# Attention loop: running maximum folded to 256 columns ahead of the last score bank, and value products placed by head

## The chip, the core and the metric

The kernel runs on one core of a Trainium2 chip. A core has five engines that run side by side, each with its own queue of instructions, and that wait for one another by semaphores: TensorE (PE in the profile; its weight loads are PEld), VectorE (DVE), ScalarE (ACT), GpSimd (POOL) and SyncE (SP, which here issues DMAs). SBUF is the working memory, PSUM the accumulator into which TensorE writes. The metric is the device time of one execution in microseconds (us), the lower the better; runs of one kernel are given by their median.

## The reference, cut to what matters

The program is a two-layer network over 1024 latent tokens and 256 context tokens. Each layer projects its input, runs four groups side by side (latent attention, a pooling mixer, a state space, a gating block) and projects the result. The change lies in the attention alone, which is this, for blocks of queries:

```python
def one(qs):
    qn, qr = qs
    s = (jnp.einsum('bqhd,bkhd->bhqk', qn, k_nope)
         + jnp.einsum('bqhr,bkr->bhqk', qr, k_rope))
    p = jax.nn.softmax(s.astype(jnp.float32) * scale, axis=-1)
    return jnp.einsum('bhqk,bkhd->bqhd', p, vf)
```

There are 4 heads with 64 value columns each. Latent queries look at all 1280 keys (10 blocks of 128), context queries (first layer only) at the 256 context keys. All is in float32.

## The kernel before

`attention` (line 1200) works on 256 queries and two heads at a time: a *pair* is one group of 256 queries with heads 0 and 1, or with heads 2 and 3. The first layer has 10 pairs, 8 of latent queries and 2 of context queries, the second layer 8. The loop at line 1465 makes one turn for each head of each pair: `v` is the pair, `h` the head in it (0 the first, 1 the second). In this text the turns are numbered through both layers: 0 to 19 in the first, 20 to 35 in the second. Turns 4, 5, 18 and 19 belong to context queries and are short (2 key blocks); the other 32 are long (10 key blocks).

Scores are kept turned: keys on the partitions, queries along the columns. A *bank* of PSUM holds 512 columns, here two key blocks of 256 queries each, so a long turn has 5 banks (`BANKS`, line 1198). The softmax needs the maximum over all keys of each query. The order of a turn, by names and lines:

- `scores` (line 1300): TensorE writes the scores bank by bank, 6 matmuls in each (line 1316, tiles `mm_sc` or `tp_sc`). The first bank of a turn is computed at the end of the turn before, and ScalarE copies it to `acc`, an SBUF tile of 128 x 512 (line 1322). For each of the other four banks VectorE takes the elementwise maximum of `acc` and the bank (line 1324; in the profile these stand under line 130, the helper that issues them, as `acc<-acc,mm_sc`). Behind the last bank VectorE folds `acc` to 256 columns: the maximum of its two halves, both in SBUF (line 1326, in the profile `acc<-acc`).
- `maxima` (line 1333): TensorE transposes the folded `acc` (line 1338, tile `tp_mx`), and VectorE reduces it to one maximum a query, `mx` (line 1340).
- `rows` (line 1342): TensorE turns `mx` back and spreads it out (line 1347, again tile `tp_mx`), and VectorE makes `row` of it in two instructions (lines 1349 and 1350; 143 and 147 in the profile).
- `shift` (line 1352): TensorE adds `row` to each score bank with one more matmul, which subtracts the maximum.
- `exps` (line 1361): ScalarE takes the exponentials of the five banks (`pE`, `pL`, `pM`), and GpSimd adds them up to `psum`: four adds of 512 columns and one fold to 256, all operands in SBUF (lines 1383 and 1384; line 130 in the profile).
- `values` (line 1388): TensorE multiplies the exponentials of the **pair before** with the values, into `av`, 64 x 256 each. There are 10 key blocks and 2 heads, so 20 such products for a pair; they are given out over the two turns of the next pair as something for TensorE to do while VectorE works on the maximum. `PVS` (line 36) says how: the 5 key blocks of a turn are cut into three pieces, put ahead of `maxima`, between `maxima` and `rows`, and between `rows` and `shift` (lines 1482 to 1489). A product of one key block and head is one matmul in the program and two records in the profile. In the first pair of a layer `att_values` stands there in their place, and `PVS` is not used; nor does it do anything where the pair before is short.

Ahead of `maxima` there may also be matmuls for the queries of the next pair (tile `tp_q`). Within the loop the order on TensorE, VectorE, ScalarE and GpSimd is the order in which the code issues (`manual_schedule`, line 1464): each engine takes its instructions strictly one after the other.

Of the kernel before, what the change touches and what calls it, by code (L numbers as in the profile page):

```python
# [16 lines left out]
ALU = mybir.AluOpType  # L17
# [15 lines left out]
NSLOT = 160  # L33
NPOS = 165
SEG = 32
PVS = ((0, 2), (2, 3), (3, 5))
VW = ((0, 1, None), (2, 3, None))
CX = 2
POW = ((0, 4), (4,))
# [35 lines left out]
def tile_hybrid_backbone(ctx: ExitStack, tc: tile.TileContext, A):  # L75
    nc = tc.nc
    V, S, P, T, D = nc.vector, nc.scalar, nc.gpsimd, nc.tensor, nc.sync
# [23 lines left out]
    def mm_ps():  # L101
        return psmm.tile([128, 512], F32, tag="mm", name="mm_" + stg[0])

    def tp_ps():
        return pstp.tile([128, 512], F32, tag="tp", name="tp_" + stg[0])
# [16 lines left out]
    def s2(name="s2", dt=F32):  # L122
        return wk.tile([128, 512], dt, tag="s2", name=name, bufs=2)
# [5 lines left out]
    def tt(e, out, a, b, op):  # L129
        return e.tensor_tensor(out=out, in0=a, in1=b, op=op)  # L130
# [1069 lines left out]
    def attention(l, last, blocks, out):  # L1200
# [5 lines left out]
        n = 256  # L1206
# [21 lines left out]
        def q_split(c0):  # L1228
            ts_ = slice(c0, c0 + n)
            cqn = (xs("cqn", F32R, 1024) if len(chunk) == 1 else hx("cqn", F32R)).rearrange("p (k e t) -> p k e t", k=2, e=2)  # L1230
            parts = [(cqn[:, 0], cq0[:, ts_]), (cqn[0:64, 1], cq1[0:64, ts_])]
            rope = None
            if c0 < NLAT:
                rope = tile_of("ropeq", F32, 2)
                D.dma_start(rope, A["rope"][:, :, ts_])
            chunk[c0] = cqn, rope
            yield "act"
            for y, x in parts:
                S.copy(y[:, 0], x)
            S.copy(cqn[64:128, 1, 0], cqn[0:64, 1, 0])  # L1240
            yield "dve"
            for y, x in parts:
                sub(P, y[:, 1], x, y[:, 0])

        def q_chunk(c0):

            cqn, rope = chunk[c0]
            yield "mm"
            stg[0] = "q"
            ps = tp_ps()  # L1250
            q_mm(ps[:, 0:n], cqn, slice(256, 384))
            if c0 < NLAT:
                q_mm(ps[:, n:2 * n], cqn, slice(384, 512))
            yield "act mm"
            qf = wl("qf", F32)
            m = 2 * n if c0 < NLAT else n
            S.copy(qf[:, 0:m], ps[:, 0:m])
            yield "row"
            if c0 < NLAT:
                mul(V, qf[:, 0:m].rearrange("p (e t) -> p e t", e=2), qf[:, 0:m].rearrange("p (e t) -> p e t", e=2), rope)  # L1260
                add(V, qf[:, 0:n], qf[:, 0:n], qf[:, n:2 * n])
            qr = tile_of("qr", F32R, 2)
            chunk[c0] = cqn, qr
            yield "act"
            S.copy(qr[:, 0], qf[:, 0:n])
            yield "dve"
            sub(V, qr[:, 1], qf[:, 0:n], qr[:, 0])
# [32 lines left out]
        def scores(v, h, banks):  # L1300

            c0, pr = pairs[v]
            stg[0] = "sc"
            K, Q = KT[2 * pr + h][(slice(0, 96), slice(0, 128))[h]], prep[v][h]
            if 0 in banks:
                st[v, h] = dict(b=[], acc=s2("acc"))
            d = st[v, h]
            acc = d["acc"]
            for i, kts in list(enumerate(BANKS if c0 < NLAT else BANKS[0:1]))[banks.start:banks.stop]:
                ps = tp_ps() if nb[0] % 6 == 5 else mm_ps()  # L1310
                nb[0] += 1
                d["b"].append(ps)
                for x, kt_ in enumerate(kts):
                    out = ps[:, n * x:n * x + n]
                    for y, (e, f) in enumerate(((0, 0), (0, 1), (1, 0))):
                        T.matmul(out, lhsT=K[:, e, 128 * kt_:128 * kt_ + 128], rhs=Q[:, f], start=(x == 0 and y == 0),  # L1316
                                 stop=False, skip_group_check=True)
                if c0 == NLAT:
                    V.tensor_reduce(out=acc[:, 0:n], in_=ps.rearrange("p (x q) -> p q x", x=2), axis=AX.X, op=ALU.max)
                    continue  # L1320
                if i == 0:
                    d["first"] = lambda: S.copy(acc, d["b"][0])
                else:
                    tt(V, acc, acc, ps, ALU.max)
                if i == 4:
                    tt(V, acc[:, 0:n], acc[:, 0:n], acc[:, n:2 * n], ALU.max)

        def first(v, h):

# [79 lines left out]
        def finish(v):  # L1409

            c0, pr = pairs[v]
            ci = min(c0 // 512, 2)
            gt = c0 - CH0[ci][0]
            gs = G[ci][:, pr, gt:gt + n]
            yield "fend"
            stg[0] = "sm"
            tp = tp_ps()
            for h in range(2):
                T.matmul(tp[64 * h:64 * h + 64, 0:n], lhsT=ones.to_broadcast([128, 64]), rhs=st[v, h]["sm"][:, 0:n],
                         start=True, stop=True, skip_group_check=True)  # L1420
            yield "fdve"
            rs = qp[0].tile([128, n], F32, tag="rs", name="rs", bufs=2) if v < nv - 1 else s2("rs")[:, 0:n]
            V.reciprocal(out=rs, in_=tp[:, 0:n])
            yield "av"
            mul(V, gs, st[v][:, 0:n], gs)
            mul(V, gs, rs, gs)
            for x in (v, (v, 0), (v, 1)):
                st.pop(x)
# [3 lines left out]
        def start(g):  # L1432
            work.append([next(g), g])

        def go(what):

            for x in list(work):
                if x[0] == what:
                    x[0] = next(x[1], None)
                    if x[0] is None:  # L1440
                        work.remove(x)
# [22 lines left out]
        with tc.manual_schedule(engines={mybir.EngineType[x] for x in MAN}):  # L1464
            for w in range(2 * nv):
                v, h = w // 2, w % 2
                short = pairs[v][0] == NLAT
                for u in fresh[1:]:
                    if w == max(2 * u - 5, 0):
                        start(q_split(pairs[u][0]))  # L1470
                go("act")
                scores(v, h, range(1, 5))
                if h == 0 and v:
                    start(finish(v - 1))
                for u in fresh[1:]:
                    if w == 2 * u - 3:
                        start(q_chunk(pairs[u][0]))
                if h == 0 and v + 1 < nv:
                    start(q_pair(v + 1, *pairs[v + 1]))
                go("mm")  # L1480
                go("act mm")
                k = [range(5 * h + i, 5 * h + j) for i, j in PVS]
                vals(v, w, k, 0)
                maxima(v, h)
                vals(v, w, k, 1)
                rows(v, h)
                go("m4")
                go("row")
                vals(v, w, k, 2)
                if h and short:  # L1490
                    go("fend")
                    go("fdve")
                if h:
                    go("av")
                if not short:
                    go("fend")
                    go("fdve")
                go("dve")
                if w == 2 * nv - 2:
                    out.y(0)  # L1500
                if w == 2 * nv - 1:
                    drop("attq", "att")
                    out.alloc()
                    out.split()
                shift(v, h)
                if w + 1 < 2 * nv:
                    scores((w + 1) // 2, 1 - h, range(0, 1))
                exps(v, h)
                if w == 2 * fresh[-1] - 3:
                    out.scales()  # L1510
                if w == 2 * nv - 4:
                    out.load()
                    out.load()
                if w == 2 * nv - 2 and short:
                    for _ in range(3):
                        out.load()

            v = nv - 1
            go("act")
            start(finish(v))  # L1520
            out.part(0)
            values(v, range(0, 4))
            out.split()
            out.part(0)
            out.load()
            out.load()
            values(v, range(4, 10))
            out.split()
            go("fend")
            go("fdve")  # L1530
            go("av")
            out.load()
            out.load()
            out.load()
            out.part(0)
            out.split()
            out.part(0)
            out.split()
            out.part(0)
# [500 lines left out]
```

## Time and profile before

| | us |
|---|---|
| median of 3 runs | 1385.57 |
| the runs | 1374.05, 1385.57, 1389.56 |
| the profiled execution, its own time | 1387.97 |
| its span, first to last instruction | 1386.2 |
| attention loop, first layer (turns 0 to 19) | about 455 to 645 |
| attention loop, second layer (turns 20 to 35) | about 1119 to 1280 |
| TensorE, VectorE, GpSimd busy over the span | 1270.6, 899.5, 412.9 |
| granted TensorE clock, mean share of full speed | 0.961 |

The profile shows one execution. A row of its timeline is: start, duration (both us), engine, line, operation, what it writes and reads, and how often; instructions of one kind that follow each other are merged into one row, whose duration goes from the first one's start to the last one's end. In brackets stands how long the engine was idle before it and who ended the wait. Matmuls overlap in the array, and their ends are modelled: a matmul may start some 0.07 us before the end that is shown for the one in front.

### The profile page before, as it was taken

Reading aid. Unit: us, or ns where it says so; the run is one execution under the profiler, and the core shown is the slowest. Engines: PE = TensorE matmul, PEld = TensorE weight load, DVE = VectorE, ACT = ScalarE, POOL = GpSimd, SP = SyncE. Lnnn points to the kernel's source line nnn. Section 1 sums busy time; section 2 is a strip of 40 time slices with the busy share of each in tenths; the row PEclk is TensorE's granted clock in tenths of the full one; section 3 lists DMA queues with packets and bytes.
Section 4 is the critical chain, followed back from the end, with each engine's and each line's share of the span. In section 5 each row is a group of like instructions: output and inputs, shape, how many; then the busy total and the mean of one; then the engine's idle time right before and its main releaser. Section 6 shows DMA issues by size and latency. Waiting matters only on the chain.

```text
span 1386.2 us, 19652 instructions
## 1 busy us (share of the span) xinstructions
PE 1270.6 (92%) x7556; PEld 977.2 (70%) x7556; DVE 899.5 (65%) x1636; ACT 475.8 (34%) x879; POOL 412.9 (30%) x418
## 2 busy tenths in 40 slices
PE   4788999999999998999999889999899999998997
PEld 1567777689788766665777767678697775665785
DVE  8778299514543576757798956699345457667756
ACT  2351311120453544445243333412223464544200
POOL 2431000001002445655434410100011235666342
PEclk9899999999999898999999989999899999999999
DMA  8446433752412000014123345522742200000421
GB/s 310 159 111 205 138 92 108 187 143 62 122 24 46 31 9 1 4 44 135 48 77 106 100 141 163 169 70 72 172 103 50 51 24 16 31 5 28 152 100 67
DMA packets 124675, 127.43 MB, mean 92 GB/s; under 512 B 40908, under 2 KB 98724, under 8 KB 124582
## 3 DMA queue, kind: packets, MB, share of 16 engines
q1 hardware_dynamic: 118886, 111.86, 27.4%
q0 software_dynamic: 2880, 9.67, 3.0%
q10 hardware_dynamic: 2816, 4.65, 0.9%
q8 instruction: 59, 0.97, 0.3%
q14 instruction: 34, 0.28, 0.1%
HBM read 97.53 MB, written 26.00 MB: 89 GB/s over the span
## 4 chain that ended last, share of the span: by engine, by line
PE 54%; DVE 28%; issue 6%; ACT 5%; POOL 4%; DMA 3%; SPq 1%; DVEq 0%; POOLq 0%; ACTq 0%
PE mm_out L1621 7%; PE mm_in L151 6%; PE mm_in L152 6%; PE mm_in L153 6%; PE mm_sc L1316 6%; PE av L1399 4%; DVE acc L130 3%; DVE H L130 3%; DVE z L147 3%; DVE stmp L130 2%; DVE op L130 2%; DVE xres L144 1%; PE mm_sc L1358 1%; DVE wlo L130 1%; PE tp_sc L1316 1%
## 5 line engine op out<-in xcount | busy, mean ns | idle before, releaser
L152 PE MATMUL mm_in<-hT,whi 128*128 128x512 f32 (+1 forms) x696 | 263.3, 379 | 4.5 <-POOL hT L130 3.4
L151 PE MATMUL mm_in<-hT,whi 128*128 128x512 f32 (+1 forms) x696 | 265.9, 383 | 0.1
L153 PE MATMUL mm_in<-hT,wlo 128*128 128x512 f32 (+1 forms) x696 | 261.2, 376 | 0.0
L1621 PE MATMUL mm_out<-wo,yh 128*128 128x512 f32 x576 | 164.2, 398 | 1.7 <-DVE wo L130 1.6
L151 PEld LDWEIGHTS mm_in<-hT,whi 128*128 128x128 f32 x696 | 133.9, 193 | 35.2 <-issue 12.2
L152 PEld LDWEIGHTS mm_in<-hT,whi 128*128 128x128 f32 x696 | 134.1, 193 | 31.5 <-POOL hT L130 6.4
L153 PEld LDWEIGHTS mm_in<-hT,wlo 128*128 128x128 f32 x696 | 133.9, 193 | 24.5 <-issue 1.6
L1621 PEld LDWEIGHTS mm_out<-wo,yh 128*128 128x128 f32 x576 | 107.4, 189 | 29.6 <-DVE wo L130 3.2
L130 DVE TENSOR_TENSOR acc<-acc,mm_sc 128x512 f32<-128x512 f32 x108 | 74.2, 687 | 44.1 <-PE mm_sc L1316 33.8
L637 ACT CAST whi<-wraw 128x1024 fp32r<-128x1024 f32 x38 | 42.6, 1122 | 167.0 <-PE mm_in L152 113.2
L1621 PE MATMUL mm_out<-wo,yl 128*128 128x512 f32 x288 | 93.0, 395 | 0.4 <-POOL yl L130 0.4
L130 POOL TENSOR_TENSOR psum<-pE 128x512 f32<-128x512 f32 (+1 forms) x36 | 46.0, 1279 | 136.9 <-ACT pE L1377 136.8
L130 POOL TENSOR_TENSOR psum<-psum,pL 128x512 f32<-128x512 f32 x64 | 83.4, 1304 | 7.7 <-ACT pL L1377 3.0
L130 DVE TENSOR_TENSOR wlo<-wraw,whi 128x1024 fp32r<-128x1024 f32 x38 | 48.5, 1276 | 37.8 <-ACT whi L637 37.8
L1621 PEld LDWEIGHTS mm_out<-wo,yl 128*128 128x128 f32 x288 | 54.3, 188 | 13.3 <-POOL yl L130 0.8
L1377 ACT ACTIVATE pE<-mm_sc 128x512 f32<-128x512 f32 x55 | 30.6, 595 | 94.3 <-PE mm_sc L1358 75.0
L130 DVE TENSOR_TENSOR H<-H,stmp 128x160 f32<-128x160 f32 (+1 forms) x140 | 59.4, 424 | 4.1
L1605 ACT CAST yh<-G 128x1024 fp32r<-128x1024 f32 x18 | 18.9, 1051 | 116.2 <-PE mm_out L1621 114.9
L1316 PE MATMUL mm_sc<-QA,KT 96*128 96x256 f32 x372 | 57.2, 311 | 0.0
L1316 PEld LDWEIGHTS mm_sc<-QA,KT 96*128 96x128 f32 x372 | 52.6, 214 | 6.4 <-issue 6.3
L143 POOL TENSOR_SCALAR rs_z<-mv_z 128x1 f32<-128x1 f32 x18 | 18.5, 1029 | 121.2 <-DVE mv_z L1653 121.2
L1772 ACT ACTIVATE G<-mm_in 128x512 f32<-128x512 f32 (+1 forms) x40 | 22.2, 556 | 85.8 <-PE mm_in L153 85.4
(348 smaller groups left out, 2628.2 us busy)
## 6 DMA issues: line engine op xcount, KB each, us to landing
wmod<-in_w_mod_dram SPq DMA_DIRECT2D x48, 512.0 KB, 4.1
wraw<-in_w_in_dram SPq DMA_DIRECT2D x36, 512.0 KB, 4.5
wor<-in_w_out_dram SPq DMA_DIRECT2D x16, 512.0 KB, 3.8
s5u<-Sd SPq DMA_DIRECT2D x8, 640.0 KB, 7.4
xd<-z SPq DMA_DIRECT2D x10, 512.0 KB, 2.7
xin<-in_x_dram SPq DMA_DIRECT2D x8, 512.0 KB, 7.3
Ed<-E ACTq DMA_DIRECT2D x16, 256.0 KB, 3.4
Eld<-Ed SPq DMA_DIRECT2D x8, 512.0 KB, 4.3
```

Source lines behind the costliest of these rows:

```text
L130: return e.tensor_tensor(out=out, in0=a, in1=b, op=op)
L147: return V.scalar_tensor_tensor(out=out, in0=a, scalar=s, in1=b, op0=op0, op1=op1)
L151: T.matmul(out, lhsT=ahi, rhs=bhi, start=start, stop=False)
L152: T.matmul(out, lhsT=ahi, rhs=blo, start=False, stop=False)
L153: T.matmul(out, lhsT=alo, rhs=bhi, start=False, stop=stop)
L637: copy(hi, raw)
L1316: T.matmul(out, lhsT=K[:, e, 128 * kt_:128 * kt_ + 128], rhs=Q[:, f], start=(x == 0 and y == 0), stop=False, skip_group_check=True)
L1377: S.activation(out=p, in_=ps, func=AF.Exp, scale=QSCALE)
L1399: T.matmul(st[v][64 * h:64 * h + 64, 0:n], lhsT=Vt[:, BANKS[i // 2][i % 2], 64 * head:64 * head + 64], rhs=st[v, h]["pt"][i // 2][:, n * ( ...
L1605: S.copy(yhv, f)
L1621: T.matmul(a[1][nh], lhsT=y[u][:, k, :], rhs=self.W[k][:, v, 512 * nh:512 * nh + 512], start=(k == 0 and u == 0 and v == 0), stop=(k == KC ...
L1772: S.activation(out=G[ci][:, b, :], in_=ps, func=AF.Silu)
```

## The change

In `scores`, the fold of `acc` to 256 columns now stands behind the third maximum (`i == 3`) and no longer behind the fourth. The last bank is then taken in by two maxima, each of the folded 256 columns of `acc` and of one half of the bank. In the table `PVS`, each head of a pair now has a row of its own. The first head's is the old one: 2, 1 and 2 key blocks. The second head's is 2, 2 and 1: one key block, two products, comes ahead of `rows` and no longer behind it.

```diff
--- before.py
+++ after.py
@@ -33,7 +33,7 @@
 NSLOT = 160
 NPOS = 165
 SEG = 32
-PVS = ((0, 2), (2, 3), (3, 5))
+PVS = (((0, 2), (2, 3), (3, 5)), ((0, 2), (2, 4), (4, 5)))
 VW = ((0, 1, None), (2, 3, None))
 CX = 2
 POW = ((0, 4), (4,))
@@ -1320,10 +1320,13 @@
                     continue
                 if i == 0:
                     d["first"] = lambda: S.copy(acc, d["b"][0])
-                else:
+                elif i < 4:
                     tt(V, acc, acc, ps, ALU.max)
+                if i == 3:
+                    tt(V, acc[:, 0:n], acc[:, 0:n], acc[:, n:2 * n], ALU.max)
                 if i == 4:
-                    tt(V, acc[:, 0:n], acc[:, 0:n], acc[:, n:2 * n], ALU.max)
+                    for x in range(2):
+                        tt(V, acc[:, 0:n], acc[:, 0:n], ps[:, n * x:n * x + n], ALU.max)
 
         def first(v, h):
 
@@ -1479,7 +1482,7 @@
                     start(q_pair(v + 1, *pairs[v + 1]))
                 go("mm")
                 go("act mm")
-                k = [range(5 * h + i, 5 * h + j) for i, j in PVS]
+                k = [range(5 * h + i, 5 * h + j) for i, j in PVS[h]]
                 vals(v, w, k, 0)
                 maxima(v, h)
                 vals(v, w, k, 1)
```

VectorE, turn 6 (line 130 is the helper of all maxima and folds; the brackets name the engines whose semaphores an instruction waits for, the number is the same for all):

```order
 L130 TENSOR_TENSOR acc<-acc,tp_sc 128x512 [waits PE_49,Activation_49]
-L130 TENSOR_TENSOR acc<-acc,mm_sc 128x512 [waits DVE_49,PE_49] x3
-L130 TENSOR_TENSOR acc<-acc 128x256 [waits DVE_49]
-L1340 TENSOR_REDUCE mx<-tp_mx 128x2 [waits PE_49]
+L130 TENSOR_TENSOR acc<-acc,mm_sc 128x512 [waits DVE_49,PE_49] x2
+L130 TENSOR_TENSOR acc<-acc 128x256 [waits DVE_49]
+L130 TENSOR_TENSOR acc<-acc,mm_sc 128x256 [waits DVE_49,PE_49]
+L130 TENSOR_TENSOR acc<-acc,mm_sc 128x256 [waits DVE_49]
+L1343 TENSOR_REDUCE mx<-tp_mx 128x2 [waits PE_49]
```

The fold has moved ahead of the last bank, whose one maximum became two; of these the first waits for TensorE, the second for VectorE alone. All 32 long turns read so.

TensorE, turn 15 (the second head of a pair), from the first value products on, before the change:

```order
L1399 MATMUL av<-pL,Vt 64x256 x4
L1338 MATMUL tp_mx<-ident,acc 128x128 x2
L1399 MATMUL av<-pL,Vt 64x256 x2
L1347 MATMUL tp_mx<-ident,mx 128x128 x2
L1399 MATMUL av<-pM,Vt 64x256 x4
L1358 MATMUL mm_sc<-row,ones_93 128x512 x4
```

And the same place in the changed kernel, where later lines have moved down by three:

```order
L1402 MATMUL av<-pL,Vt 64x256 x4
L1341 MATMUL tp_mx<-ident,acc 128x128 x2
L1402 MATMUL av<-pL,Vt 64x256 x2
L1402 MATMUL av<-pM,Vt 64x256 x2
L1350 MATMUL tp_mx<-ident,mx 128x128 x2
L1402 MATMUL av<-pM,Vt 64x256 x2
L1361 MATMUL mm_sc<-row,ones_93 128x512 x4
```

Two of the four products behind the second transposes have moved ahead of them. This is so in 15 turns, the second heads of those pairs whose pair before is long. No other instruction of any engine has moved.

## Rows read from the trace of the kernel before

**Rows 1.** The page: busy time of each engine, and the chain by engine.
```profile
PE 1270.6 (92%) x7556; PEld 977.2 (70%) x7556; DVE 899.5 (65%) x1636; ACT 475.8 (34%) x879; POOL 412.9 (30%) x418
...
PE 54%; DVE 28%; issue 6%; ACT 5%; POOL 4%; DMA 3%; SPq 1%; DVEq 0%; POOLq 0%; ACTq 0%
```

**Rows 2.** Waits, whole span: waiter <- releaser: us in total, times, longest.
```profile
PE tp_mx L1338 <- DVE acc L130: 16.8, 13, 2.1
...
PEld tp_mx L1347 <- DVE mx L1340: 13.9, 32, 0.8
```

**Rows 3.** Instructions on tile acc: count: ns least/median/most, first and last start.
```profile
L130 DVE TENSOR_TENSOR acc<-acc,mm_sc x108: 673/687/690, 454.9 to 1272.2; 128x512 f32<-128x512 f32 x108
...
L130 DVE TENSOR_TENSOR acc<-acc x32: 424/554/1519, 458.0 to 1272.9; 128x256 f32<-128x256 f32 x32
```

**Rows 4.** VectorE's groups by form, 455 to 645: count | busy us, mean ns.
```profile
L130 DVE TENSOR_TENSOR G<-av,G 128x256 f32<-128x256 f32 x9 | 3.7, 408 | 1.3 <-PE av L1399 1.3
```

**Rows 5.** Timeline, turn 10 (a first head).
```profile
553.35 3.06 DVE L130 TENSOR_TENSOR acc<-acc,mm_sc 128x512 f32<-128x512 f32 x4 [1.44 <-PE mm_sc L1316]
...
554.03 2.65 POOL L130 TENSOR_TENSOR psum<-psum,pL 128x512 f32<-128x512 f32 x2
...
556.10 1.08 PE L1399 MATMUL av<-pE,Vt 128*64 128x256 f32 x8
...
556.45 0.52 DVE L130 TENSOR_TENSOR acc<-acc 128x256 f32<-128x256 f32 x1
...
557.11 0.44 PE L1338 MATMUL tp_mx<-ident,acc 128*128 128x128 f32 x2
```

**Rows 6.** Timeline, turn 8 (a first head).
```profile
533.92 0.69 DVE L130 TENSOR_TENSOR acc<-acc,tp_sc 128x512 f32<-128x512 f32 x1 [0.35 <-PE tp_sc L1316]
...
534.43 1.28 POOL L130 TENSOR_TENSOR psum<-psum,pM 128x512 f32<-128x512 f32 x1
...
535.44 0.56 DVE L130 TENSOR_TENSOR acc<-acc 128x256 f32<-128x256 f32 x1
...
536.31 0.44 PE L1338 MATMUL tp_mx<-ident,acc 128*128 128x128 f32 x2
```

**Rows 7.** Timeline, turn 9 (a second head).
```profile
542.59 2.72 POOL L130 TENSOR_TENSOR psum<-psum,pL 128x512 f32<-128x512 f32 x2
542.72 2.26 DVE L130 TENSOR_TENSOR acc<-acc,mm_sc 128x512 f32<-128x512 f32 x3
...
545.08 0.69 DVE L130 TENSOR_TENSOR acc<-acc,tp_sc 128x512 f32<-128x512 f32 x1
...
545.39 1.26 POOL L130 TENSOR_TENSOR psum<-psum,pM 128x512 f32<-128x512 f32 x1
545.80 1.13 DVE L130 TENSOR_TENSOR acc<-acc 128x256 f32<-128x256 f32 x1
...
547.08 0.62 PE L1338 MATMUL tp_mx<-ident,acc 128*128 128x128 f32 x2 [2.11 <-DVE acc L130]
```

**Rows 8.** Timeline, turn 15 (a second head), from the first transposes on.
```profile
607.44 0.41 PE L1338 MATMUL tp_mx<-ident,acc 128*128 128x128 f32 x2
...
607.78 0.65 PE L1399 MATMUL av<-pL,Vt 128*64 128x256 f32 x4
607.89 0.43 DVE L1340 TENSOR_REDUCE mx<-tp_mx 128x2 f32<-128x256 f32 x1 [0.59 <-PE tp_mx L1338]
...
608.37 0.43 PE L1347 MATMUL tp_mx<-ident,mx 128*128 128x128 f32 x2
...
608.73 1.08 PE L1399 MATMUL av<-pM,Vt 128*64 128x256 f32 x8
...
609.36 0.48 DVE L147 SCALAR_TENSOR_TENSOR row<-tp_mx,par,row 128x256 fp32r<-128x256 f32 x1
...
609.90 0.51 PE L1358 MATMUL mm_sc<-row,ones 2*128 2x512 f32 x4
```

**Rows 9.** Windows, core 0: us, busy time (count) of PE, PEld, DVE, ACT, POOL, PEclk.
```profile
547.05:551.00 3.95, 3.92 (x20) 1.70 (x20) 1.39 (x3) 0.00 (x0) 1.83 (x3) 0.57 0.00 0
```

## The prediction

> **What bounds the kernel now.** I read the page first. TensorE is busy for 92% of the span and has 54% of the chain that ended last; VectorE has 28% of that chain [rows 1]. So what counts is time in which TensorE stands still for VectorE. The waits view names two such places in the attention loop: the transposes of the running maximum wait for `acc` (16.8 us in 13 turns), and the weight load of the transposes that spread the maximum out waits for `mx` (13.9 us in 32) [rows 2]. The first is what the edit in `scores` touches, the second what the edit of `PVS` touches. I number the loop's turns as the kernel does: 0 to 19 in the first layer, and on from there, 20 to 35, in the second; 32 of the 36 are long (ten key blocks), four are short.
>
> The timeline of single turns then shows who is late. After the last score matmul TensorE has value products to do, while VectorE finishes the maxima and the fold; then TensorE can transpose. In turn 10 the fold ends at 556.45 + 0.52 = 556.97 and the products at 556.10 + 1.08 = 557.18; the transposes start at 557.11, without a wait [rows 5]. In turn 9 the fold ends at 546.93, the transposes start at 547.08, and TensorE had stood for 2.11 us [rows 7]. In neither does VectorE wait for the last bank: its maxima run back to back (four of 0.687 in 3.06 us, three in 2.26, so 0.10 apart). VectorE is the late engine in this tail.
>
> The row that decides the case is how long a fold takes: 424 ns at least, 554 in the median, 1519 at most, for one and the same shape [rows 3]. GpSimd's adds beside it show why. Turn 10: two adds on `psum` end at 554.03 + 2.65 = 556.68, the fold at 556.97 [rows 5]. Turn 8: the add ends at 535.71, the fold at 536.00 [rows 6]. Turn 9: 546.65 and 546.93 [rows 7]. The fold ends 0.28 to 0.29 us behind the add that was running when it started, however long that add still had; so it is in all 27 turns where a fold starts in an add with more than 0.1 us to go. The maxima, with one input in PSUM, take 673 to 690 ns always [rows 3]. The fold reads two SBUF operands and so does the add: they exclude each other, and the fold waits out the whole add.
>
> **The change, part by part.**
>
> *The last bank's maximum in two halves.* One 512-wide maximum (0.687) becomes two of 256 in each of 32 turns. The trace has this form under another name, `G<-av,G`, 256 columns, one input in PSUM: 408 ns [rows 4]; I take 0.41. Between two of them stand 0.10, as between the maxima above; between fold and first half 0.04 (the fold's own distance, 545.08 + 0.69 to 545.80 [rows 7]) to 0.10, say 0.07. That is 0.99 behind the fold. By the order's waits the first half waits for TensorE and the second for VectorE alone, so neither starts before the bank is whole. The Trainium skill, "VectorE: DVE Perf Modes", section on the TRN2 errata, speaks against this edit: each instruction pays a fixed latency, so it wants 512 elements or more. Its formula (N + 151)/0.96 gives an estimate of 424 ns a half, by which the sum would be about 1 us higher than by the row.
>
> *The fold moves ahead of the last maximum.* It would be hidden if VectorE then waited for the last bank, but VectorE doesn't. So the new tail is: end of the third maximum, fold, two halves, and what the fold costs there hangs on the add that runs at that moment. I went through the 32 long turns with the end of the third maximum, GpSimd's adds, and the end of what covers TensorE.
>
> Turn 10 [rows 5]: the fourth maximum takes the last 0.69 before 556.41, the third ends 0.10 ahead of it, at 555.62, so the fold would start at 555.66. The second `pL` add runs to 556.68; the fold ends at 556.97, as it does now, although it starts 0.8 us sooner. The halves end 0.99 later, at 557.96; the transposes start 0.15 behind (as in turn 9) at 558.11, not at 557.11: **+1.00**. Turns 12, 15, 24, 26, 32, 33 and 34 are alike: eight, +8.0. Turn 8 [rows 6]: third maximum to 534.61, add to 535.71, fold to 536.00, halves to 536.99, transposes at 537.14 and not 536.31: **+0.83**; turns 2, 14, 22 and 28 have +0.77, +0.90, +0.74 and +0.83: five, +4.1.
>
> Turn 9 [rows 7]: the third maximum ends at 544.98, the fold would start at 545.02. The second of the two adds from 542.59 ends at 545.31, so the fold ends at 545.59, the halves at 546.58, and the transposes start at 546.73, not at 547.08: **-0.35**. Now the fold starts just behind the next add (545.39) and waits out all of it; then it would catch the end of the one ahead. Turns 3, 13, 17, 23, 25, 27, 31 and 35 are alike: nine, -3.2.
>
> In turns 0, 1, 6, 16, 20, 21 and 30 the fold meets no add, or the tail of one as now; free, the tail goes from 0.10 + 0.69 + 0.04 + 0.42 = 1.25 to 0.04 + 0.42 + 0.99 = 1.45, partly covered: +1.2. In turns 7, 11 and 29 other matmuls cover all of it: 0. Sum: 8.0 + 4.1 - 3.2 + 1.2 = +10.1 us; with 0.04 or 0.10 ahead of the halves, 9.2 to 11.0.
>
> *Value products.* In 15 second heads of a pair two products move from behind the second transposes to ahead of them. Turn 15 [rows 8]: transposes of `acc` at 607.44, four records of products from 607.78 (0.65 us), `mx` done at 608.32, second transposes at 608.37, `row` done at 609.84, shift at 609.90. That chain has no slack: the second transposes start 0.05 behind `mx`, the shift 0.06 behind `row`. Eight records take 1.08 in place of 0.65, so the second transposes, queued behind them on TensorE, start 0.43 later, and `row` and the shift follow. Behind the transposes there were eight records and are then four, but TensorE waits for `row` either way. What the edit fills ahead of them (rows 2, the wait for `mx`) opens again at the shift: **+0.43** in 11 turns, 4.7. In turns 9, 13, 23 and 27 TensorE ran at a lower clock (granted 0.57, near the lower of its levels, 1.2 of 2.4 GHz, after turn 9's stop [rows 9]) and its own products were partly the limit, so there 0 to 0.45 each; 0.8 together. Sum 5.5, bounds 4.7 and 6.5.
>
> *Total:* 10.1 + 5.5 = 15.6, bounds 13.9 and 17.5. No instruction of GpSimd, ScalarE or a DMA queue moves. A delayed turn starts the next one later, since the next scores stand behind the shift on TensorE, and GpSimd's adds follow the exponentials behind the same shift, so the phases above repeat. Against the profiled 1388.0 this gives 1403.6; the median of the three runs is 2.4 lower, which gives 1401.2. I say **1402**.
>
> **Rivals.**
>
> *The fold is not held in its new place.* Then it costs 0.42 anywhere. The nine turns like 9 gain 0.50 (fold to 545.44, halves to 546.43 in place of 546.93): -4.5; the eight like 10 lose 0.11: +0.9; the five like 8 nothing; the rest +1.2; products +5.5: +3.1, 1390, no change. It decides if most folds stay under 0.45 us. For it: 424 ns is seen. Against: every fold that met an add ended behind it. The Trainium skill, "SBUF — State Buffer", section "Who interferes with whom", says that of two such instructions the first to issue keeps the shared port and the other fully blocks; by that rule this rival is out, and the trace agrees (0.28 us behind the add).
>
> *The clock pays it back.* From transposes to shift turns 9 and 23 take 3.8 us and turns 13 and 27 2.9, where 2.46 is normal (607.44 to 609.90 [rows 8]). If stops of 1.76 us in place of 2.11 no longer cost clock, 3.7 us come back: 1398. With the fold not held either, and the products free, it would be 3.1 - 5.5 - 3.7 = -6.1, 1381, the only gain I see. Against: the change adds stops of 0.7 to 1.0 us in thirteen turns.
>
> *The phase slips.* In the turns like 9 the fold starts 0.29 us before the running add ends. If VectorE is later by that much, the fold meets the next add (1.26 us), and the nine turns go from -0.35 to +0.99: 12 us more, 1414.
>
> **How the numbers follow.** Forecast 0.70 (its own range 1396 to 1408), clock 0.10, not held 0.11, slip 0.06, gain 0.03. The range reaches to the not-held case and the slip: 1386 to 1414. A measurement of this kernel can tell about 1%, 14 us, from no change. The forecast lies just on that bound, so it splits: slower by over 1% 0.52, within 1% 0.44, faster 0.04.
>
> **What would show it.** In the profile of the changed kernel folds should still end 0.28 us behind an add, with a median above 0.7 us; 256-wide maxima take 0.41 to 0.42; TensorE's waits for `acc` go from 13 turns to some 25 and from 17 to about 27 us; the second transposes of second heads stop waiting for `mx`, and the shift there comes 2.9 us behind the first transposes, not 2.46. I am wrong if folds of 0.42 prevail, if GpSimd's adds start at other places between the maxima, or if the shift still comes at 2.46.

## The result

The changed kernel takes 1393.51 us (median of 15 runs, 1390.36 to 1400.1), the kernel before 1385.87 (median of 15, 1374.05 to 1390.94). The ratio is 1.0065, with a 95% interval of 1.0045 to 1.0086: some 9 us slower (7.6 by the medians), and clear of noise, but within 1%. The profiled executions differ by 7.9 us in their spans.

The page after: busy time and the chain by engine; of before they are [rows 1].

```profile
PE 1268.0 (91%) x7556; PEld 973.9 (70%) x7556; DVE 910.2 (65%) x1668; ACT 475.6 (34%) x879; POOL 412.7 (30%) x418
...
PE 52%; DVE 29%; issue 5%; ACT 5%; DMA 4%; POOL 4%; SPq 1%; DVEq 0%; POOLq 0%; ACTq 0%
```

Tile `acc` after, its folds alone (ns least/median/most, then us from first to last; before, [rows 3]):

```profile
L130 DVE TENSOR_TENSOR acc<-acc x32: 424/1294/1405, 458.5 to 1281.7; 128x256 f32<-128x256 f32 x32
```

The waits after, of TensorE for the folded maximum, of its shift for `row`, and of its weight loads for `mx` (us in all, waits, the longest; before, the first and the last are [rows 2]):

```profile
PE tp_mx L1341 <- DVE acc L130: 25.3, 22, 1.8
...
PE mm_sc L1361 <- DVE row L147: 7.9, 12, 1.1
...
PEld tp_mx L1350 <- DVE mx L1343: 7.3, 17, 0.8
```

The wait of the shift for `row` before:

```profile
PE mm_sc L1358 <- DVE row L147: 3.3, 3, 1.1
```

The same 32 folds, with the same data, take 1294 ns in the median and not 554. TensorE waits 25.3 us for them in 22 turns (16.8 in 13 before). The wait for `mx` has fallen from 13.9 to 7.3 us, and that of the shift for `row` has grown from 3.3 to 7.9. Turn 10 shows the first effect; this is its timeline after, with start in us, duration, engine and line (before, [rows 5]):

```profile
556.48 2.65 POOL L130 TENSOR_TENSOR psum<-psum,pL 128x512 f32<-128x512 f32 x2
556.58 1.48 DVE L130 TENSOR_TENSOR acc<-acc,mm_sc 128x512 f32<-128x512 f32 x2
...
558.10 1.32 DVE L130 TENSOR_TENSOR acc<-acc 128x256 f32<-128x256 f32 x1
...
559.52 0.87 DVE L130 TENSOR_TENSOR acc<-acc,mm_sc 128x256 f32<-128x256 f32 x2
...
560.54 0.41 PE L1341 MATMUL tp_mx<-ident,acc 128*128 128x128 f32 x2 [0.90 <-DVE acc L130]
```

The fold starts at 558.10, GpSimd's adds end at 559.13, the fold at 559.42, the halves at 560.39; TensorE stood 0.90 us where it did not stand before. The timeline after of turn 9, one of the nine that gain (before, [rows 7]):

```profile
546.36 2.71 POOL L130 TENSOR_TENSOR psum<-psum,pL 128x512 f32<-128x512 f32 x2
...
548.77 0.57 DVE L130 TENSOR_TENSOR acc<-acc 128x256 f32<-128x256 f32 x1
...
549.45 0.87 DVE L130 TENSOR_TENSOR acc<-acc,tp_sc 128x256 f32<-128x256 f32 x2
...
550.47 0.41 PE L1341 MATMUL tp_mx<-ident,acc 128*128 128x128 f32 x2 [1.74 <-DVE acc L130]
```

Here the fold catches the end of the add ahead (549.07) and TensorE's stop is 1.74 us in place of 2.11. Turn 15 shows the second edit, again in the timeline after (before, [rows 8]):

```profile
611.35 0.41 PE L1341 MATMUL tp_mx<-ident,acc 128*128 128x128 f32 x2 [0.91 <-DVE acc L130]
...
611.69 0.65 PE L1402 MATMUL av<-pL,Vt 128*64 128x256 f32 x4
611.80 0.42 DVE L1343 TENSOR_REDUCE mx<-tp_mx 128x2 f32<-128x256 f32 x1 [0.59 <-PE tp_mx L1341]
612.17 0.60 PE L1402 MATMUL av<-pM,Vt 128*64 128x256 f32 x4
612.71 0.43 PE L1350 MATMUL tp_mx<-ident,mx 128*128 128x128 f32 x2
...
614.24 0.51 PE L1361 MATMUL mm_sc<-row,ones 2*128 2x512 f32 x4 [0.52 <-DVE row L147]
```

`mx` is done at 612.22, but the second transposes stand behind four more records and start at 612.71; the shift comes 2.89 us behind the first transposes, where it was 2.46, and TensorE now waits 0.52 us for `row`.

Per turn, the timelines of the two kernels differ like this (us, summed over the turns named in the forecast):

| | forecast | before to changed |
|---|---|---|
| last score matmul to transposes: eight turns like 10 | +8.0 | +7.8 |
| five turns like 8 | +4.1 | +3.5 |
| nine turns like 9 | -3.2 | -3.3 |
| the other long turns | +1.2 | +1.2 |
| transposes to shift, 15 second heads | +5.5 | +3.6 |
| transposes to shift, all other turns | 0 | -0.6 |
| shift to the last score matmul of the next turn | 0 | -3.95 |
| sum | +15.6 | +8.3 |

So the stops ahead of the first transposes are there (9.2 us of the 10.1), and 7 us of the sum are missing: 2.5 between the transposes and the shift (turns 9 and 23 are 0.95 us **shorter** there), and 4 in a place that the edits don't touch, the scores: those of turns 14 and 28 take 2.4 us less than before.

### The profile page after: what moved, and what is told of

It reads as the page before. It is cut to its first block, busy times and chain, and to the rows that moved or that the text cites. A ratio compares the mean times of both kernels' runs of the same rounds, so it can differ in the third digit from the quotient of the medians.

```text
span 1394.1 us, 19669 instructions
## 1 busy us (share of the span) xinstructions
PE 1268.0 (91%) x7556; PEld 973.9 (70%) x7556; DVE 910.2 (65%) x1668; ACT 475.6 (34%) x879; POOL 412.7 (30%) x418
## 4 chain that ended last, share of the span: by engine, by line
PE 52%; DVE 29%; issue 5%; ACT 5%; DMA 4%; POOL 4%; SPq 1%; DVEq 0%; POOLq 0%; ACTq 0%
PE mm_out L1624 7%; DVE acc L130 6%; PE mm_in L151 6%; PE mm_in L152 6%; PE mm_in L153 6%; PE mm_sc L1316 4%; PE av L1402 3%; DVE H L130 3%; DVE z L147 3%; DVE stmp L130 2%; DVE op L130 2%; DMA wmod<-in_w_mod_dram 2%; DVE xres L144 1%; PE mm_sc L1361 1%; PE tp_s5rd L872 1%
## 5 line engine op out<-in xcount | busy, mean ns | idle before, releaser
L130 DVE TENSOR_TENSOR acc<-acc,mm_sc 128x512 f32<-128x512 f32 (+1 forms) x136 | 78.5, 577 | 43.6 <-PE mm_sc L1316 31.8
```

## Experiments

**Each edit alone.** e1 is the changed kernel with the old table for both heads:

```diff
-PVS = (((0, 2), (2, 3), (3, 5)), ((0, 2), (2, 4), (4, 5)))
+PVS = (((0, 2), (2, 3), (3, 5)), ((0, 2), (2, 3), (3, 5)))
```

> The changed kernel with the old table of value products: the fold stands ahead of the last bank, its maximum is in two halves, nothing else. Theory A (the fold is held by GpSimd's add, and the change's loss is the fold's place plus the products, with some clock given back): TensorE stops ahead of the first transposes grow by about 9 us as in the changed kernel, the fold's median is near 1.3 us, the way from the first transposes to the shift stays at 2.46 in full-clock second heads; low-clock stretches after turns like 9 mostly vanish because the stop is 1.75 and not 2.11 us (about -4 to -6): in all +3 to +5 us, ratio 1.002 to 1.004. Rival B (clock does not depend on this): +9 us, 1.0065, all of the loss. Rival C (the products carry the whole loss, the fold is neutral): ratio 1.000, with folds held or not.

e2 is the kernel before with the new table alone:

```diff
-PVS = ((0, 2), (2, 3), (3, 5))
+PVS = (((0, 2), (2, 3), (3, 5)), ((0, 2), (2, 4), (4, 5)))
...
-                k = [range(5 * h + i, 5 * h + j) for i, j in PVS]
+                k = [range(5 * h + i, 5 * h + j) for i, j in PVS[h]]
```

> The kernel before with only the new table of value products. Theory A: 0.43 us in each of 13 to 15 second heads between the first transposes and the shift (2.88 in place of 2.46), +5.6 to +6.5 us, ratio 1.004 to 1.0047, with the folds as before (median 0.55 us) and stops of 2.11 us in turns like 9, so also the same low-clock stretches; if the products placed ahead also keep the clock up behind the stop, up to 4 us less. Rival C (the products carry the whole loss): +9 us, 1.0065. Rival D (the wait for the maximum is filled for nothing): 1.000 or less.

Measured: e1 1.0057 (1.0030 to 1.0083), e2 1.0021 (0.9995 to 1.0046). The fold loses by itself, more than theory A's 1.002 to 1.004 and near rival B's 1.0065. The products' loss is smaller than forecast (1.004 to 1.0047), and its interval reaches 1.0, so by the time alone they could be free. The two sum to 0.78%, the change to 0.65%. Rival C, that the products carry it all, is out; against D, that they are free, stands the profile: in e2 the way from transposes to shift is 0.42 to 0.44 us longer in nine turns (3, 11, 15, 19, 25, 29, 31, 33 and 35), with folds as before. In e1 the wait for `acc` is that of the changed kernel, in the view of the waits:

```profile
PE tp_mx L1341 <- DVE acc L130: 25.9, 22, 1.8
```

and so are the folds, in e1's view of tile `acc`:

```profile
L130 DVE TENSOR_TENSOR acc<-acc x32: 424/1304/1516, 459.5 to 1285.9; 128x256 f32<-128x256 f32 x32
```

What I had said of the clock in e1 was wrong: its profile has lower clock behind turns 9, 13, 17, 27 and 31, no fewer than the four of the kernel before, though its stops are the shorter ones of 1.75 us. e2's has it behind 9, 13, 17, 23 and 27. The changed kernel has it, of these turns, behind 27 alone in one profile, and behind 9 and 23 in a second (e8, the same kernel once more, 1.0064, 1.0040 to 1.0089). Behind turn 35 it stands in e2 and in both profiles of the changed kernel, but there it begins only 2.5 to 3 us behind the shift, when the loop is over.

> The changed kernel once more, unedited, for a second profile: theory A has the stops of the first transposes and the folds as in its first profile to 0.1 us a turn, while the low-clock stretches behind turns 9, 13, 17, 23, 27 and 31 may stand in other turns; at 1.75 us of stop there should be fewer than behind the stops of 2.1 us. Ratio 1.005 to 1.009.

**The hold by GpSimd.** In e3 and e4 one add per long turn stays, and adds ones, so that the softmax sums are not the reference's; the other three are left out.

```diff
-                for i in range(1, 5):
-                    add(P, sm, pt[0] if i == 1 else sm, pt[i])
+                for i in range(1, 2):
+                    add(P, sm, pt[0], ones.to_broadcast([128, 512]))
```

e3 is this in the kernel before, e4 in e1's.

> The kernel before with three of GpSimd's four 512-wide adds a long turn left out (the one that stays adds ones to the first exponentials), so the softmax sums are not the reference's; all else is the same. Theory A (fold held by the running add): every fold takes 0.42 us, since the one add and the 256-wide one are over by then; nine turns like 9 gain 0.7 us, about -6 us, and with their shorter stops (1.4 in place of 2.1) up to -6 us of clock: ratio 0.991 to 0.996. Rival E (folds are long for another reason, say the write of the maximum just in front): folds stay at a median of 0.55 and a most of 1.1 to 1.5 us, ratio 1.000.

> The fold ahead of the last bank and the halves (as in e1), with the three GpSimd adds left out as in e3. Theory A: the fold takes 0.42 us in its new place too; against e3 the tail is longer by 0.1 to 0.2 us a long turn (two halves for one maximum), +2 to +4 us, where the same edit costs some 9 us of stops when the adds are there. Rival E (the place itself costs): the same +9 us of stops against e3 as e1 has against the kernel before.

Measured: e3 0.9848 (0.9812 to 0.9885), e4 0.9867 (0.9835 to 0.9900). Tile `acc` of e3, its folds (least/median/most ns), and behind it e3's wait of TensorE for them:

```profile
L130 DVE TENSOR_TENSOR acc<-acc x32: 424/425/922, 460.5 to 1255.0; 128x256 f32<-128x256 f32 x32
```

```profile
PE tp_mx L1338 <- DVE acc L130: 8.9, 10, 1.5
```

The same two views of e4:

```profile
L130 DVE TENSOR_TENSOR acc<-acc x32: 424/425/770, 458.6 to 1256.6; 128x256 f32<-128x256 f32 x32
```

```profile
PE tp_mx L1341 <- DVE acc L130: 8.8, 10, 1.7
```

With the adds gone the fold takes 425 ns in the median in either place, so it was the adds that held it. The four longer ones in e3 (0.86 to 0.92 us) and the one in e4 (0.77) end 0.28 us behind another GpSimd instruction (`cqn<-raw,cqn`) that was running. Moving the fold costs 2.2 us from the last score matmul to the transposes (sum over the long turns, e3 to e4), where the same edit costs 9.9 with the adds (before to e1). Rival E is out. e3 gained some 21 us where I expected 6 to 12: its timeline has no lower clock behind turns 9 to 19 or 22 to 35 any more, and the subtraction on `qr`, which had taken 1.28 us in the median, takes 0.56.

**The clock.** To see what the lower clock takes, TensorE was given something to do in the seven long stops (turns 9, 13, 17, 23, 27, 31 and 35, which an added helper `late` names): matmuls of no use, ahead of the first transposes. e5 is this in the kernel before, e6 in the changed one.

```diff
+                if late(v, h):
+                    for x in range(7):
+                        T.matmul(st[v - 1][0:64, n:2 * n], lhsT=Vt[:, 0, 0:64], rhs=st[v - 1, 1]["pt"][0][:, 0:n],
+                                 start=False, stop=False, skip_group_check=True)
                 maxima(v, h)
```

> The kernel before with seven matmuls of no use (64 x 256, as a value product, into unused columns of av) ahead of the first transposes in turns 9, 13, 17, 23, 27, 31 and 35, where TensorE stands for 2.1 us. They take 1.5 us of a stop that VectorE sets, so the instructions behind start no later. Theory A (those stops bring the lower granted clock, and the profile before lost some 8 us by that in turns 9, 13, 14, 23, 27 and 28): granted clock 1.00 behind these turns, time down by 4 to 9 us, ratio 0.994 to 0.997. Rival B (the clock falls there for another reason): the stretches stay and the ratio is 1.000 or more.

> The changed kernel with the same seven idle matmuls in the same turns. Theory A (the forecast's 15.6 us of added waits are all there, and the changed kernel got 5 to 7 us back because its stops in these turns are 1.75 and not 2.11 us, with less low clock): against e5 it is slower by 14 to 16 us, so 1.006 to 1.007 of the kernel before, with no low clock behind these turns in either. Rival F (the added waits are smaller than reckoned in most runs): against e5 it is slower by 9 us only, as the changed kernel is against the one before.

e5 came out at 0.9986 (0.9960 to 1.0012), and not 0.994 to 0.997. The timeline of turn 9 in e5 says why:

```profile
547.27 3.19 PE L1492 MATMUL av<-pE,Vt 128*64 128x256 f32 x14
...
550.39 0.44 PE L1344 MATMUL tp_mx<-ident,acc 128*128 128x128 f32 x2
```

The row has 14 records for the seven matmuls; they start 0.215 us apart, so one matmul takes 0.43, where a value product takes 0.21. Value products write the two halves of `av` by turns, 64 partitions each, and these all wrote the same half; that this makes the difference is my reading, and no run here tries it alone. The seven overran the stop and put the transposes 0.8 us later in six turns and 1.2 in turn 35, which ate the gain. e6 was 1.0110 (1.0076 to 1.0143), 15.9 us above e5, but with the gain of these seven turns (of the nine like 9) covered in both. So both once more with three:

```diff
-                    for x in range(7):
+                    for x in range(3):
```

> As e5, with three idle matmuls in place of seven: in e5 each took 0.42 us, not the 0.21 that a value product takes beside its partner in the other half of av, so seven overran the stop and put the first transposes 0.84 us later in seven turns, which covered the gain. Three take 1.26 us and end at 2.3 us behind the last score matmul, ahead of the fold (3.0), so no instruction starts later. Theory A: granted clock 1.00 behind turns 9 to 31, first transposes at 3.1 as before, time down by 4 to 9 us, ratio 0.994 to 0.997. Rival B (the clock has no part in it): 1.000.

> The changed kernel with the three idle matmuls. Theory A (the forecast's waits are all there and the lower clock hid a part of them): against e9 it is slower by 13 to 16 us (first transposes +9 to +10.5, products +0.43 in 15 turns, 6.4, less 0.2 us in a few first turns), with no low clock behind turns 9 to 31 in either, that is 1.004 to 1.007 of the kernel before. Rival F (the waits are smaller than reckoned): against e9 it is slower by 9 us.

Measured: e9 0.9937 (0.9906 to 0.9968), 1377.20 us; e10 1.0047 (1.0024 to 1.0071), 1393.08 us. Between them lie **15.9 us** by the medians, 15.2 by the ratios, good to some 3 us by the spread of the runs; without the idle matmuls it was 7.6 and 9.0. In the loop neither profile has lower clock behind turns 9 to 20 or 22 to 34, and turn by turn the two timelines differ by 9.5 us from the last score matmul to the transposes, by 6.0 from there to the shift in the 15 second heads, and by -0.6 there in the others: 14.9 us of added waits, where 15.6 were forecast. (Over all executions e10 has a mean clock of 0.968 and e9 of 0.970, so a little of the 15.9 is clock.) Windows from the transposes of turn 13 to those of 15, 23 to 24, and 27 to 29 show where: us, busy time of PE, PEld, DVE, ACT, POOL, then the granted clock. Before:

```profile
586.52:607.44 20.92, 20.74 (x132) 14.73 (x133) 12.82 (x21) 9.07 (x18) 11.94 (x12) 0.84 0.14 51
1154.25:1164.29 10.04, 10.04 (x65) 6.50 (x65) 5.50 (x10) 4.02 (x9) 6.00 (x7) 0.83 0.00 0
1194.02:1215.90 21.88, 21.71 (x138) 15.44 (x138) 12.73 (x21) 9.30 (x18) 12.89 (x12) 0.84 0.15 49
```

Changed:

```profile
590.97:611.35 20.38, 17.83 (x132) 12.43 (x133) 14.49 (x23) 9.06 (x18) 13.21 (x12) 1.00 0.16 52
1159.48:1169.55 10.07, 8.60 (x65) 6.08 (x65) 6.37 (x11) 4.32 (x9) 7.28 (x7) 1.00 0.05 18
1199.93:1221.48 21.55, 20.37 (x137) 13.66 (x138) 14.58 (x23) 9.29 (x18) 13.21 (x12) 0.92 0.16 49
```

e9, the kernel before with three idle matmuls a stop, and e10, the changed kernel with them:

```profile
587.84:605.86 18.02, 17.76 (x132) 12.40 (x132) 12.70 (x21) 9.08 (x18) 11.95 (x12) 1.00 0.20 59
1150.39:1159.04 8.65, 8.56 (x64) 6.07 (x65) 5.52 (x10) 4.02 (x9) 6.02 (x7) 1.00 0.00 0
1188.78:1207.78 19.00, 18.74 (x138) 13.17 (x138) 12.72 (x21) 9.27 (x18) 12.94 (x12) 1.00 0.16 56
```

```profile
591.51:611.88 20.37, 17.82 (x132) 12.43 (x133) 14.47 (x23) 9.07 (x18) 13.19 (x12) 1.00 0.16 52
1157.68:1167.76 10.08, 8.60 (x65) 6.08 (x65) 6.37 (x11) 4.32 (x9) 7.30 (x8) 1.00 0.07 28
1198.14:1218.53 20.39, 18.80 (x138) 13.17 (x138) 14.49 (x23) 9.29 (x18) 13.22 (x13) 1.00 0.16 52
```

The kernel before ran these turns at a mean of 0.83 to 0.84, and e9, which only has more to do in the stops, at 1.00 (2.4 GHz) and 2.9, 1.4 and 2.9 us faster. The busy time of TensorE tells the same: 20.74 us for the same 132 records that take 17.76 (17.83 in the changed kernel). The changed kernel is slower than e9 in all three windows (by 2.4, 1.4 and 2.5 us, the last with some lower clock of its own), and yet no slower than the kernel before, since that one paid about as much in clock. At 1.00 in both, e10 is slower than e9 by 2.4, 1.4 and 1.4.

A profile is one execution, but the granted clock is on record for nearly all. The 65 executions of the kernel before that ran beside e1 to e10 have a mean of 0.963, the 25 of the changed kernel 0.966 (standard errors under 0.001); e1 and e2, 12 executions each, have 0.963 and 0.962. In each of the three sets of the kernel before, an execution with 0.001 less clock took 1.1 us more. So over all executions the changed kernel gets some 4 us back in clock, give or take 2; the 7 us of the two profiles is more than the usual. And neither edit alone raises the clock.

**A tail that GpSimd can't hold.** e7 is the kernel before, without a fold in the same seven turns: TensorE transposes all 512 columns, and VectorE reduces them from PSUM.

```diff
-                if i == 4:
+                if i == 4 and not late(v, h):
                     tt(V, acc[:, 0:n], acc[:, 0:n], acc[:, n:2 * n], ALU.max)
...
+            if late(v, h):
+                for j in range(4):
+                    T.transpose(tp[:, 128 * j:128 * j + 128], d["acc"][:, 128 * j:128 * j + 128], ident)
+                V.tensor_reduce(out=m, in_=tp.rearrange("p (x j k) -> p j x k", x=2, j=2), axis=AX.XY, op=ALU.max)
+                return
```

> The kernel before, without a fold in turns 9, 13, 17, 23, 27, 31 and 35: there TensorE transposes all 512 columns of the running maximum (four transposes in place of two) and VectorE reduces 512 columns from PSUM, which GpSimd cannot hold. Theory A: the first transposes start at 2.0 us behind the last score matmul and not at 3.1; the way to the shift grows by 0.5 (two transposes, 0.27 us more in the reduction), so 0.6 us a turn, -4 us; and a stop of 1.0 in place of 2.1 us leaves the clock up, -4 to -8: ratio 0.991 to 0.995. Rival E (the fold is long for another reason than GpSimd's add): the tail is not shorter than 0.4 us, ratio 0.999 to 1.002.

Measured: 1373.16 us, 0.9896 (0.9861 to 0.9930), faster than either kernel. Turn 13:

```profile
578.21 0.65 PE L1346 MATMUL tp_mx<-ident,acc 128*128 128x128 f32 x4 [0.86 <-DVE acc L130]
...
578.90 0.69 DVE L1347 TENSOR_REDUCE mx<-tp_mx 128x2 f32<-128x512 f32 x1 [0.75 <-PE tp_mx L1346]
579.12 0.72 POOL L130 TENSOR_TENSOR psum<-psum 128x256 f32<-128x256 f32 x1
579.65 0.43 PE L1358 MATMUL tp_mx<-ident,mx 128*128 128x128 f32 x2 [0.20 <-DVE mx L1347]
```

The stop is 0.86 us and no longer 2.1, and the larger reduction costs 0.27 of it again. In all seven turns the reduction takes 691 to 693 ns, though in six of them, as here, it begins in one GpSimd instruction and ends in the next, so it isn't held as the fold was. The first transposes come 1.1 to 1.4 us sooner, the shift 0.5 later behind them (in turns 17, 31 and 35, which are at full clock in both), about 5 us over seven turns. The rest goes with the clock, which is at 1.00 behind turns 9 to 33 (the mean over all executions is 0.970, 0.962 for the kernel before beside it); how the 14 us divide between the two no run tells apart.

## Why the prediction was right and wrong

*The hold: right.* I read from 27 folds that a fold ends 0.28 us behind the running add, and that in its new place it would meet an add in thirteen covered turns. It did: turn 10 +0.97 (forecast +1.00), turn 9 -0.37 (-0.35), and in the changed kernel's profile again 27 folds end 0.28 to 0.29 us behind a GpSimd instruction. e3 and e4 show that it is the adds. Two sizes were off a little: the two halves stand 0.03 apart, not 0.10 (0.87 us for both), and turn 8 lost nothing: in the changed kernel's profile its scores ran at the lower clock nearly throughout, and the add that holds the fold stands earlier against them (it starts 0.7 us ahead of the last score matmul, where before it started 0.1 behind). The rivals "not held" and "the phase slips" did not occur.

*The halves: right.* 420 ns at least; nothing was hidden behind the last bank.

*The products: right in kind, a little low.* 0.43 us in most second heads. The 0.8 that I set for turns 9, 13, 23 and 27 is 1.7 at full clock: e9 to e10 has 6.0 us over the 15 turns, where 5.5 were forecast. In turn 5 it is only 0.15.

*The sum: right for the waits, too high for the time.* Of the forecast's 15.6 us of waits 14.9 stand in the timelines of e9 and e10; in time they lie 15.9 apart, and that this comes within 0.3 of the forecast is partly luck, at an uncertainty of 3. Without the idle matmuls it is 7.6 to 9. What I had wrong is the clock: the sum put it at nothing, and the rival "the clock pays it back" stood at 3.7 us and a chance of 0.10, as a thing that shorter stops might bring. I had measured the lower clock only from the transposes to the shift, in turns 9, 13, 23 and 27. In turns 13 and 27 it ran on into the scores of turns 14 and 28: from the shift to the end of the last score matmul it took 6.85 and 6.93 us there, where 4.4 to 4.5 is normal. The window of the kernel before over the end of turn 13 and the scores of 14 (granted clock 0.50) shows it:

```profile
588.09:594.92 6.83, 6.83 (x33) 5.25 (x30) 2.38 (x6) 3.15 (x6) 2.81 (x4) 0.50 0.22 77
```

With it the profile before held about 8.5 us of lower clock (by e9's turns 1.37 us in turn 9, 1.39 in 23, 0.50 in 13, 0.43 in 27, and 2.42 and 2.47 in the scores of 14 and 28), more than half of the forecast's loss, ready to be given back. The changed kernel keeps a smaller part of it. So the time fell 8.5 us short of the forecast, within the range of 1386 to 1414, but below the forecast's own 1396 to 1408, and on the "within 1%" side, to which I had given 0.44. That the range holds it is luck in part: its lower end was set for folds that are not held, and they are held. That case was also reckoned a little high: 1385.6 and its 3.1 us give 1389, not 1390.

*What stays open.* Why the changed kernel has less of the lower clock, I can't say. Its stops are shorter, but e1's are as short and e1's profile had lower clock behind five of these turns; it also has twice the products just behind the first transposes, but e2 has those as well. The granted clock of all executions bears out that only both edits together raise it (0.966, against 0.963 for the kernel before and for e1 and 0.962 for e2), and not why.

## What to carry to other kernels

Before moving a two-operand SBUF operation of VectorE, lay GpSimd's instructions beside its new place: its cost there is the rest of the GpSimd instruction that runs at that moment (here with 0.28 us on top), and it may be cheaper to give it an operand in PSUM, as e7 does. Moving filler from one wait to another on the same dependency chain only moves the stop. And before adding up waits, look at the granted clock of every stretch of the stage, the scores included: where a kernel already pays for its stops in clock, a change that makes it wait elsewhere can be partly paid for by that.

## What was not expected

Three idle matmuls in each of seven stops, 1.3 us of work that yields nothing, made the kernel before 0.6% faster (e9). And a product of 64 x 256 took 0.43 us when one after the other wrote the same half of `av`, and 0.21 in the value products, which write the two halves by turns.
